# Seven block products in one load of four of the 16-tile products, and running maxima by a matmul

## The chip, the cores and the metric

The kernel runs on one core of a Trainium2 chip. Its metric is the time of one execution in microseconds (us), given as the median of several runs. A core has five engines with instruction queues of their own: PE (TensorE, matmuls), DVE (VectorE), ACT (ScalarE), POOL (GpSimd) and SP (SyncE, which here issues the weight loads). Each engine works its queue in order; semaphores make one wait for another.

## The reference

A decoder trunk of two layers over 256 tokens of width 2048, in float32.

```
xn    = rms_norm(h, g)
q, k, v, o, ig, fg = split(xn @ w_in)               # 8 heads; q, k 128 wide, v, o 256
hh    = mlstm_chunkwise(q, k, v, softcap(ig), log_sigmoid(softcap(fg)))
        # weights exp(dmat - m_t), m_t a running maximum over the tokens;
        # rows divided by max(|sum|, exp(-m_t))
h     = h + (rms_norm(hh, w_hnorm) * sigmoid(o)) @ w_out
h     = h + (silu(conv(up)) * conv(up2)) @ w_down   # gated FFN, width 5632
q     = rope(rms_norm(h, gb) @ w_q);  k, v = split(rms_norm(h, gkv) @ w_kv)
o     = (softmax(q1 k1) - lam * softmax(q2 k2)) @ v # causal, 8 heads, v 256 wide
h     = h + (rms_norm(o, g_subln) * (1 - lambda_init)) @ w_o
h     = h + FFN(h);  out = rms_norm(h, final_norm)
```

The products with "tokens out", which the change is about, are the v and o parts of `xn @ w_in`, `@ w_out`, the v part of `@ w_kv`, and `@ w_o`. Each has 2048 rows of weights, 16 k-tiles of 128, and 2048 columns of output.

## The kernel before

**Arithmetic.** Every float32 operand is split into a high and a low half, `x = xh + xl`, and a product is three matmuls: high by high, low by high, high by low. Weights come from memory as `raw` tiles of one megabyte (four k-tiles of 512 columns; `RAW` = 4 slots). A `granule` takes half of such a tile: ACT copies the high half into a `w2` tile (L375), DVE subtracts it for the low half (L376). There are `HL` = 5 slots for `w2`; a slot comes free when PE has done with the granule in it.

**Products.** `gemm` computes q, k and the FFN's up projections, with columns out. `gemm_tokens` (matmul L436) computes the products with tokens out, in groups of 512 columns: two accumulator banks for a group, one for each 128 tokens, and 16 k-tiles in eight granules of 12 matmuls of 512 columns. `acc_ps` has four accumulator banks, so that two groups can be under way; the other four banks of PSUM (`small_ps`) serve everything small: scores `s_ps`, head outputs `val_ps`, transposes `hn_ps`, `an_ps`, `turn_ps`, and the `mix` banks below. After its last matmul a group is evacuated: `evac_v` scales and splits the values of two heads (`mv`, `av`: ACT L305, DVE L306), `evac_o` multiplies the head rows by the gate, `residual` adds to the residual stream.

**Seven products for eight.** The down projection of the FFN has a second form, `gemm_sevenths` (matmuls L493, ordinary granules L503): for two of the five full loads in each group (a half of the FFN's width is 22 k-tiles) the 2 x 2 block product of (two halves of the tokens, two k-tiles) by (two k-tiles, two column halves) is made with seven block products instead of eight, after Winograd. It needs differences of weight blocks (`sevenths`, DVE L448 to L450, kept in a `diff` tile that takes a slot of `raw`), passes over three and four blocks (L457, L458), four mixed operands for each pair of k-tiles (`mix`, made where the hidden operands are made), and two `mix` banks beside the two accumulators. The sums in the mix banks are added to the stream afterwards by `mixed_in`.

**Heads.** In `mlstm` a head's weights are made in `weights(h)`: scores by L728 and L729, the causal mask minus the running maximum on DVE (L722), three exponentials on ACT (L724 to L726), multiplication by the scores (L730). The running maximum `top[h]` is a row of `mx` that a DMA from POOL's queue broadcasts to 128 partitions (L680), eight of them. `weighted` multiplies with the values (`val_ps`, L334); ACT sums squares (`sq`), DVE and POOL take the inverse root (`rsqrt`: two seeds on DVE, L270 and L271, then three Newton steps of four operations on POOL, L278 to L281), and ACT scales the rows (`hn` in the gated layer, `nrm` in the attention, L347). `turn` transposes them on PE (`hn_ps`, `an_ps`) for the operands of the output projection (`mo`, `ao`).

**Order.** The program is written as Python code in which `later(n, ...)` puts a head's steps behind the n-th next granule (`tick`); from that code a scheduler with a model of the engines' times sets the final order on every engine. The numbers behind names below are buffer numbers.

## Time and profile before

| | |
|---|---|
| median of 3 runs | 2272.68 us (2271.36 to 2272.86) |
| the profiled execution | 2271.45 us, of which the span 2269.6 |
| granted PE clock, mean | 0.997 |
| PE, PEld busy | 2249.4 us, 1948.0 us |
| DVE, ACT, POOL busy | 1699.5 us, 1269.7 us, 120.7 us |
| DMA moved | 420.04 MB, mean 185 GB/s |

PE is busy when a matmul is under way, PEld when PE loads the stationary operand; the two overlap. In a row of a group, "out<-in" are the tiles by the program's names, then counts, busy time and mean, and the engine's idle time ahead with what ended it. The gated layer's products v and o run from about 109 to 304 us of the span, its output projection to about 397, the first FFN to about 1140, the attention's v from 1327 to 1420, its output projection to about 1535, then the second FFN.

### The profile page before, as it was taken

How to read it: one execution, taken by the hardware profiler on the slowest of the kernel's cores; microseconds unless marked ns; L12 is line 12 of the kernel's file. 1: busy time of each engine (PE TensorE's matmuls, PEld its weight loads, DVE VectorE, ACT ScalarE, POOL GpSimd, SP SyncE). 2: the span in 40 equal slices, each digit the busy share in tenths (PEclk: the TensorE clock that was granted, in tenths of full speed). 3: DMA queues.
4: the chain of work that ended last, by engine and by line, in shares of the span. 5: the costliest groups of instructions: out<-in, count | busy, mean ns of one | idle time of the engine just before them, and what ended most of it. 6: DMA issues, size and time to landing. Idle time of an engine off the chain costs nothing.

```text
span 2269.6 us, 32658 instructions
## 1 busy us (share of the span) xinstructions
PE 2249.4 (99%) x12574; PEld 1948.0 (86%) x12574; DVE 1699.5 (75%) x2769; ACT 1269.7 (56%) x1940; POOL 120.7 (5%) x313
## 2 busy tenths in 40 slices
PE   9989999999999999999999999999999999999998
PEld 9868888888888888888888888888888888888888
DVE  6746555778788877788888885567787887787885
ACT  5446544656655555566654556556565555555554
POOL 0013100000000000000012102200000000000000
PEclk9999999999999999999999999999999999999999
DMA  7774555555545755555565555455555466555464
GB/s 264 142 197 161 181 180 182 188 186 186 190 167 185 235 187 186 186 170 183 192 213 188 167 167 167 167 182 181 190 189 186 158 204 214 189 189 191 146 213 149
DMA packets 325728, 420.04 MB, mean 185 GB/s; under 512 B 9198, under 2 KB 238916, under 8 KB 325572
## 3 DMA queue, kind: packets, MB, share of 16 engines
q1 hardware_dynamic: 325156, 416.89, 55.8%
q0 software_dynamic: 384, 1.05, 1.4%
q8 instruction: 99, 1.62, 0.3%
q14 instruction: 57, 0.47, 0.1%
q10 hardware_dynamic: 32, 0.01, 0.0%
HBM read 414.77 MB, written 2.10 MB: 184 GB/s over the span
## 4 chain that ended last, share of the span: by engine, by line
PE 97%; DMA 2%; DVE 0%; ACT 0%; issue 0%; DVEq 0%; ACTq 0%
PE acc L410 53%; PE acc L436 20%; PE acc L503 13%; PE mix L493 4%; PE acc L493 3%; PE acc L594 2%; DMA raw<-in_m_w_in_dram 2%; PE val_ps L334 1%; PE acc L521 1%; PE turn_ps L230 1%; PE as_ps L915 0%; PE gps L641 0%; PE as_ps L916 0%; PE hn_ps L356 0%; PE an_ps L356 0%; PE warm_ps L129 0%
## 5 line engine op out<-in xcount | busy, mean ns | idle before, releaser
L376 DVE TENSOR_TENSOR w<-raw,w 128x1024 fp32r<-128x1024 f32 x708 | 860.1, 1220 | 402.4 <-ACT w L375 398.1
L375 ACT ACTIVATE w<-raw 128x1024 fp32r<-128x1024 f32 x708 | 747.8, 1058 | 596.1 <-PE acc L410 349.3
L410 PE MATMUL acc<-x_f,w 128*128 128x512 f32 (+1 forms) x5632 | 987.9, 337 | 0.0
L410 PEld LDWEIGHTS acc<-x_f,w 128*128 128x128 f32 x5632 | 862.3, 188 | 123.1
L503 PE MATMUL acc<-w,hid 128*128 128x512 f32 x1260 | 299.7, 394 | 0.0
L503 PEld LDWEIGHTS acc<-w,hid 128*128 128x128 f32 x1260 | 233.7, 188 | 52.7
L436 PE MATMUL acc<-w,x_a 128*128 128x512 f32 x768 | 185.8, 399 | 9.1 <-ACT w L375 9.1
L410 PE MATMUL acc<-x_at,w 128*128 128x256 f32 (+1 forms) x1024 | 182.2, 338 | 0.0
L436 PEld LDWEIGHTS acc<-w,x_a 128*128 128x128 f32 x768 | 143.2, 189 | 42.7 <-ACT w L375 9.5
L410 PEld LDWEIGHTS acc<-x_at,w 128*128 128x128 f32 x1024 | 156.8, 188 | 22.4 <-ACT x_at L305 0.3
L416 ACT ACTIVATE low<-acc 128x256 f32<-128x256 f32 x216 | 79.1, 384 | 134.1 <-PE acc L410 134.1
L457 ACT ACTIVATE w<-diff 128x1024 fp32r<-128x1024 f32 x60 | 63.6, 1060 | 92.0 <-PE acc L503 47.4
L417 DVE TENSOR_TENSOR acc<-acc,low 128x256 f32<-128x256 f32 x216 | 84.0, 429 | 40.4 <-ACT low L416 40.3
L796 ACT ACTIVATE c<-u,conv 128x256 f32<-128x256 f32 x176 | 97.9, 593 | 3.5 <-DVE u L794 3.2
L458 DVE TENSOR_TENSOR w<-diff,w 128x1024 fp32r<-128x1024 f32 x60 | 73.2, 1221 | 33.7 <-ACT w L457 33.7
L899 POOL TENSOR_TENSOR sw<-sw,sin_t 32x256 f32<-32x256 f32 x32 | 41.8, 1322 | 1050.3 <-DVE sw L898 1026.6
L436 PE MATMUL acc<-w,ao 128*128 128x512 f32 x384 | 92.0, 396 | 0.0
L436 PE MATMUL acc<-w,x_at 128*128 128x512 f32 x384 | 92.0, 396 | 0.0
L436 PE MATMUL acc<-w,mo 128*128 128x512 f32 x384 | 91.5, 397 | 0.0
L436 PEld LDWEIGHTS acc<-w,mo 128*128 128x128 f32 x384 | 71.4, 188 | 16.7
L436 PEld LDWEIGHTS acc<-w,ao 128*128 128x128 f32 x384 | 71.3, 188 | 16.3
L436 PEld LDWEIGHTS acc<-w,x_at 128*128 128x128 f32 x384 | 71.3, 188 | 16.2
(263 smaller groups left out, 2012.9 us busy)
## 6 DMA issues: line engine op xcount, KB each, us to landing
raw<-in_w_up_dram SPq DMA_DIRECT2D x176, 1024.0 KB
raw<-in_w_down_dram SPq DMA_DIRECT2D x79, 1024.0 KB
raw<-in_m_w_in_dram SPq DMA_DIRECT2D x46, 1024.0 KB
raw<-in_w_kv_dram SPq DMA_DIRECT2D x32, 1024.0 KB
raw<-in_m_w_out_dram SPq DMA_DIRECT2D x16, 1024.0 KB
raw<-in_w_q_dram SPq DMA_DIRECT2D x16, 1024.0 KB
raw<-in_w_o_dram SPq DMA_DIRECT2D x16, 1024.0 KB
raw<-in_w_down_dram SPq DMA_DIRECT2D x15, 512.0 KB
```

Source lines behind the costliest of these rows:

```text
L375: act.activation(w2[:, :hc, 0], part, AF.Copy)
L376: dve.tensor_tensor(w2[:, :hc, 1], part, w2[:, :hc, 0].bitcast(F32), op=ALU.subtract)
L410: pe.matmul(to, a, b, start=(k == 0 and o == 0), stop=(k == kn - 1 and o == len(ops) - 1))
L416: act.activation(low, p[:, T:], AF.Copy)
L417: dve.tensor_tensor(p[:, :T], p[:, :T], low, op=ALU.add)
L436: pe.matmul(ps[t], a[:, s], b, start=(k == 0 and o == 0), stop=(k == kn - 1 and o == 2))
L457: act.activation(w2[:, :n, 0], src, AF.Copy)
L458: dve.tensor_tensor(w2[:, :n, 1], src, w2[:, :n, 0].bitcast(F32), op=ALU.subtract)
L493: pe.matmul(to, u, v, start=start and o == 0, stop=end and o == 2 and to is not a and to is not b, skip_group_check=True)
L503: pe.matmul(ps, u[:, s], v, start=(k0 + i == 0 and o == 0), stop=(k0 + i == kn - 1 and o == 2), skip_group_check=True)
L594: pe.matmul(ps[j], a, b, start=(k == 0 and o == 0 and j % 2 == 0), stop=(k == KD - 1 and o == 2), skip_group_check=True)
L796: act.activation(c, u, AF.Identity, bias=cw[:, 3, f:f + 1], scale=cw[:, 2, f:f + 1])
```

## The change

1. The products v, o, `w_out` and the attention's v go through `gemm_sevenths`, with one load of four k-tiles in seven products: the last load (k-tile 12 on, `MIX_AT[:1]`) for v, o and the attention's v, the third (`OUT_AT[:1]`, k-tile 8 on) for `w_out` and for the last two groups of `w_o`. The first two groups of `w_o` stay in `gemm_tokens`.
2. The operands of that load are mixed: `mix` and a new `mix_scaled` in the normalisation (`Norm.scaled`) and where `mo` and `ao` are made.
3. In v, o and the attention's v the mix banks are added back into the accumulators by a new `mixed_up`, one ACT and six DVE operations, ahead of the evacuation. `residual` uses `mixed_in` as before.
4. The eight broadcasts are gone. The negated maxima of the eight heads stay in rows 0 to 7 (high halves) and 32 to 39 (low halves) of a tile `nm`; `weights(h)` picks a head's row and spreads it with one matmul by `both_r` into a small bank `w_ps`, from which the mask addition and the first exponential read.

Of the 42 matmuls of a load in seven products 18 go into the accumulators and 24 into the two `mix` banks, which are taken from the same four small banks as `w_ps`, `s_ps` and two `val_ps`.

```diff
-            for h in range(HEADS):
-                if h % 2 == 0:
-                    top[h:h + 2] = block(F32, f"top{h // 2}")[:2]
-                nc.gpsimd.dma_start(top[h], mx[h:h + 1].rearrange("p (o t) -> p o t", o=1).broadcast_to([1, P, T]))
+            nm = block(F32R, "nm")[0]
+            pool.memset(nm.bitcast(F32), 0.0)
+            dve.tensor_scalar(nm[:8], mx, -1.0, None, op0=ALU.mult)
+            dve.scalar_tensor_tensor(nm[32:40], mx, -1.0, nm[:8].bitcast(F32), op0=ALU.mult, op1=ALU.subtract)
...
         def weights(h):
             wt = block(F32, "wt")[2][:, :384]
+            w_ps = small_ps("w_ps")[:, :T]
+            pe.matmul(w_ps, both_r[:, h:h + 1].broadcast_to([P, P]), rows["nm"], start=True, stop=True)
...
-            act.activation(wt[:, P:T], top[h][:, P:], AF.Exp, bias=c[:, h:h + 1], scale=-1.0)
+            act.activation(wt[:, P:T], w_ps[:, P:], AF.Exp, bias=c[:, h:h + 1])
...
+    def mixed_up(ps, mix):
+        (a, b), (c, d) = ps, mix
+        u = tmp("mx")
+        x, y = block(F32, "mixed_a"), block(F32, "mixed_b")
+        act.activation(x[1], c[:, :T], AF.Copy)
+        dve.tensor_tensor(u, c[:, T:], x[1], op=ALU.add)
+        dve.tensor_tensor(y[1], d[:, T:], u, op=ALU.add)
+        dve.tensor_tensor(x[0], d[:, :T], u, op=ALU.add)
+        dve.tensor_tensor(y[0], d[:, :T], y[1], op=ALU.add)
+        dve.tensor_tensor(a, a, x[2], op=ALU.add)
+        dve.tensor_tensor(b, b, y[2], op=ALU.add)
...
-        def evac_v(g, ps):
+        def evac_v(g, ps, mix):
+            mixed_up(ps, mix)
...
-        gemm_tokens(xs, w, 2 * HQK, range(4), evac_v)
-        gemm_tokens(xs, w, 2 * HQK + HV, range(4), evac_o)
+        gemm_sevenths(xs, norm.mixed, w, 2 * HQK, range(4), evac_v, MIX_AT[:1])
+        gemm_sevenths(xs, norm.mixed, w, 2 * HQK + HV, range(4), evac_o, MIX_AT[:1])
...
-    gemm_tokens(outs, w_o[0], 0, range(NG), residual(norm_f1), lead=2)
+    gemm_tokens(outs, w_o[0], 0, range(2), residual(norm_f1), lead=2)
+    gemm_sevenths(outs, outs_mixed, w_o[0], 0, range(2, NG), residual(norm_f1), OUT_AT[:1])
```

`mix` itself (four DVE differences, one ACT copy, one DVE low half) is moved, not changed. Lines below L37 move down: L376 becomes L382, L436 in the new form L508, L493 becomes L498, L306 L312, L347 L353.

**What the scheduler makes of it.** The place is the start of the first o group, where the last v group ends. On PE before, the scores of a head stand there, then the granules of the group, each in a `w2` tile of its own slot (2221, 2236 and 2294 lie in three slots):

```order
L728 MATMUL s_ps_2207<-mq3_786,mk3_1248 128x256
L729 MATMUL s_ps_2207<-mq3_786,mk3_1248 128x128
L436 MATMUL acc_2217<-w2_2221,x_a_0_172 128x512 x3
L436 MATMUL acc_2218<-w2_2221,x_a_0_172 128x512 x3
L436 MATMUL acc_2217<-w2_2221,x_a_1_175 128x512 x3
L436 MATMUL acc_2218<-w2_2221,x_a_1_175 128x512 x3
L436 MATMUL acc_2217<-w2_2236,x_a_2_244 128x512 x3
L436 MATMUL acc_2218<-w2_2236,x_a_2_244 128x512 x3
```

Now PE there (`acc_2081` is of the last v group, `acc_2391` and `acc_2392` of the first o group):

```order
L498 MATMUL acc_2081<-w2_2275,x_a_15_650 128x256 x3
L762 MATMUL w_ps_2103<-nm_1003,both_r_116 128x256
L770 MATMUL s_ps_2109<-mq2_811,mk2_1177 128x256
L771 MATMUL s_ps_2109<-mq2_811,mk2_1177 128x128
L508 MATMUL acc_2391<-w2_2395,x_a_0_174 128x512 x3
L508 MATMUL acc_2391<-w2_2395,x_a_1_177 128x512 x3
L508 MATMUL acc_2392<-w2_2395,x_a_0_174 128x512 x3
L508 MATMUL acc_2392<-w2_2395,x_a_1_177 128x512 x3
L508 MATMUL acc_2391<-w2_2430,x_a_2_246 128x512 x2
L508 MATMUL acc_2392<-w2_2430,x_a_2_246 128x512 x2
L340 MATMUL val_ps_2151<-mv4_0_2060,st4_2113 128x258 x2
```

The 18 products of the last v group into its accumulators are ahead of this piece, its 24 products into the mix banks come only after granule 2430; until then the four `w2` tiles 2266, 2269, 2272 and 2275 stay held, and 2395 and 2430 lie in one and the same slot. `acc_2391` and `acc_2392` are the banks that v group 2 had (`acc_1769`, `acc_1770`).

On ACT now, from the evacuation of v group 2 (`mv4`, `mv5`) to the pass for granule 2430:

```order
L311 ACTIVATE mv5_0_2070<-acc_1769,rt_582 128x256
L311 ACTIVATE mv5_1_2073<-acc_1770,rt_582 128x256
L353 ACTIVATE hn3_2099<-val_ps_1988,yh_2014 128x256
L353 ACTIVATE hn3_2099<-val_ps_1992,yh_2014 128x256
L766 ACTIVATE wt_2102<-w_ps_2103,c_col_1031 128x128
L767 ACTIVATE wt_2102<-wt_2102,c_col_1031 128x128
L768 ACTIVATE wt_2102<-wt_2102,c_col_1031 128x128
L381 ACTIVATE w2_2430<-raw_2393 128x2x512
```

The rows of head 3 (`hn3`, which wait for POOL's root) and the exponentials of the next head are ahead of the pass, as they were ahead of another granule's pass before; the granule behind them is now the one that PE needs next.

On DVE before, v group 2 was evacuated in the middle of group 3, between the passes of its second and third loads:

```order
L376 TENSOR_TENSOR w2_2042<-raw_2025,w2_2042 128x2x512
L306 SCALAR_TENSOR_TENSOR mv4_0_1912<-acc_1683,rt_567,mv4_0_1912 128x256
L306 SCALAR_TENSOR_TENSOR mv4_1_1915<-acc_1684,rt_567,mv4_1_1915 128x256
L722 TENSOR_TENSOR wt_1935<-mask_s_126,top2_981 128x2x128
L376 TENSOR_TENSOR w2_2076<-raw_2074,w2_2076 128x2x512
L306 SCALAR_TENSOR_TENSOR mv5_0_1922<-acc_1683,rt_567,mv5_0_1922 128x256
```

Now it stands behind the last seven-product pass of group 3 (w2_2275), and the sums of the mix banks are ahead of it:

```order
L464 TENSOR_TENSOR w2_2275<-diff_2262,w2_2275 128x4x256
L558 TENSOR_TENSOR mx_2050<-mix_1947,mixed_a_2051 128x256
L382 TENSOR_TENSOR w2_2395<-raw_2393,w2_2395 128x2x512
L782 COPY den_2004<-val_ps_1988 128x1
L559 TENSOR_TENSOR mixed_b_2052<-mix_1948,mx_2050 128x256
L560 TENSOR_TENSOR mixed_a_2051<-mix_1948,mx_2050 128x256
L782 COPY den_2004<-val_ps_1992 128x1
L561 TENSOR_TENSOR mixed_b_2052<-mix_1948,mixed_b_2052 128x256
L562 TENSOR_TENSOR acc_1769<-acc_1769,mixed_a_2051 128x512
L783 TENSOR_TENSOR den_2004<-den_2004 128x2
L563 TENSOR_TENSOR acc_1770<-acc_1770,mixed_b_2052 128x512
L784 TENSOR_TENSOR den_2004<-den_2004,e2m_1032 128x2
```

The four splits of `mv4` and `mv5` follow behind this piece, with the two seeds of head 3's root (`yh_2014`) among them.

## The prediction

> **What bounds the kernel now.** I read the page's first and fourth parts, then the waits of PE, then the chain of waits.

> ```profile
> PE 2249.4 (99%) x12574; PEld 1948.0 (86%) x12574; DVE 1699.5 (75%) x2769; ACT 1269.7 (56%) x1940; POOL 120.7 (5%) x313
> PE 97%; DMA 2%; DVE 0%; ACT 0%; issue 0%; DVEq 0%; ACTq 0%
> L376 DVE TENSOR_TENSOR w<-raw,w 128x1024 fp32r<-128x1024 f32 x708 | 860.1, 1220 | 402.4 <-ACT w L375 398.1
> PE acc L436 <- ACT w L375: 9.1, 1, 9.1
> 96.12 37.48 DMA raw<-in_m_w_in_dram
> 133.70 1.06 ACT w L375
> 134.81 1.22 PE acc L436 x2
> ```

> PE is the bound: 97% of the chain and one wait worth the name, 9.1 us. There a weight load of the gated layer takes 37.48 us, the ACT pass follows it, and PE the pass. Whatever takes work off PE is gained in full, unless DVE or ACT then make PE wait. DVE's largest group is a pass of 1.22 us over every weight granule, and DVE sat idle before those passes because ACT, and before ACT the PE, had not released a slot: it has slack, on average 25%.

> **Term 1, the eight broadcasts.** The rows below are the DMA queues from 85 to 135 us, the broadcasts' time to landing, and windows around the stall (span, then busy us of PE, PEld, DVE, ACT, POOL; PEclk; DMA share; GB/s).

> ```profile
> q0 software_dynamic: 384, 1.05, 63.6%
> top<-gate POOLq DMA_DIRECT2D x8, 128.0 KB, 21.8
> 95.00:124.00 29.00, 29.00 (x147) 24.14 (x146) 11.69 (x21) 7.78 (x11) 3.94 (x15) 1.00 0.98 55
> 126.00:128.00 2.00, 0.00 (x0) 0.00 (x0) 0.00 (x0) 0.00 (x0) 0.00 (x0) 0.96 0.92 99
> 128.00:136.00 8.00, 1.19 (x2) 0.50 (x2) 1.21 (x2) 2.00 (x2) 0.00 (x0) 0.50 0.89 268
> 138.00:140.00 2.00, 2.00 (x10) 1.64 (x9) 1.82 (x2) 1.40 (x3) 0.00 (x0) 0.98 1.02 363
> 134.81 5.46 PE L436 MATMUL acc<-w,x_a 128*128 128x512 f32 x15 [9.09 <-ACT w L375]
> ```

> From 95 to 124 us the DMA engines are 98% busy and move 55 GB/s; once the broadcasts are through they move 363. One megabyte in small packets took the engines from the weight loads. Without them nothing is left at this place that PE would wait for, so the 9.1 us go. The granted clock fell to 0.50 in the idle stretch and was still there when PE resumed: 15 matmuls took 5.46 us. At the warm pace below (0.2327 us) they are 3.49, so another 2.0 us go. Term 1: -11.1 (bounds 0, if the load is late for another reason, and -11.1; I take the gain, since the q0 row is the only thing that differs from the windows after). The replacement, a memset, two small DVE operations and eight matmuls of 256 columns, is priced in term 2.

> **Term 2, PE's work.** The down projection already runs such products; its PE timeline:

> ```profile
> 655.59 11.33 PE L503 MATMUL acc<-w,hid 128*128 128x512 f32 x48
> 666.76 0.53 PE L493 MATMUL mix<-w,hid 128*128 128x256 f32 x3
> 671.73 5.72 PE L503 MATMUL acc<-w,hid 128*128 128x512 f32 x24
> 677.29 0.52 PE L493 MATMUL mix<-w,hid 128*128 128x256 f32 x3
> ```

> 48 matmuls of 512 columns take 666.76 - 655.59 = 11.17 us, 0.2327 each. A load of four k-tiles is 24 of them, 5.58 us, or 42 of 256 columns, 671.73 - 666.76 = 4.97. Saved: 0.61 a load, one load in each group: 4 groups of v, 4 of o, 4 of the first output projection, 4 of the attention's v, 2 of its output projection, 18 in all: -11.0. The eight maxima matmuls cost 8 x 0.118 = 0.9. Term 2: **-10.1**. Terms 1 and 2: **-21.2**.

> **Term 3, what DVE and ACT must do more.** Durations from the down projection and from the gated layer (busy us and mean ns behind the bar):

> ```profile
> L448 DVE TENSOR_TENSOR diff<-raw 128x1024 f32<-128x1024 f32 x30 | 36.6, 1219 | 0.4 <-DMA raw<-in_w_down_dram 0.2
> L449 DVE TENSOR_TENSOR diff<-raw,diff 128x512 f32<-128x512 f32 x30 | 20.6, 685 | 0.3
> L458 DVE TENSOR_TENSOR w<-raw,w 128x768 fp32r<-128x768 f32 x60 | 57.1, 951 | 0.8 <-ACT w L457 0.8
> L458 DVE TENSOR_TENSOR w<-diff,w 128x1024 fp32r<-128x1024 f32 x60 | 73.2, 1221 | 33.7 <-ACT w L457 33.7
> L547 DVE TENSOR_TENSOR stream<-acc,stream 128x512 f32<-128x512 f32 x40 | 25.8, 682 | 0.1
> L533 DVE TENSOR_TENSOR mixed<-mix,mixed 128x256 f32<-128x256 f32 x15 | 6.3, 417 | 0.0
> L306 DVE SCALAR_TENSOR_TENSOR mv<-acc,rt,mv 128x256 fp32r<-128x256 f32 x16 | 7.3, 480 | 0.7 <-ACT mv L305 0.4
> 184.00:208.00 24.00, 24.00 (x116) 19.96 (x115) 14.44 (x30) 15.55 (x34) 8.91 (x35) 1.00 0.48 152
> 1019.00:1140.00 121.00, 121.00 (x702) 106.05 (x701) 103.62 (x132) 74.69 (x101) 0.00 (x0) 1.00 0.58 192
> 1327.00:1350.00 23.00, 23.00 (x115) 19.16 (x114) 20.13 (x44) 11.75 (x23) 2.76 (x4) 1.00 0.46 150
> ```

> A group adds on DVE: differences 1.22 + 2 x 0.685 = 2.6; passes 2 x (0.95 + 1.22) instead of 2 x 1.22, 1.9; adding the mixed banks back (L558 to L563) 4 x 0.42 + 2 x 0.68 = 3.0; together 7.5 us in v, o and the attention's v. In a v stage DVE goes from 14.44 to about 22 of 24 us, 91%; in the attention's v, where it has 20.13 of 23, above 100% for one group. The down projection ran at 103.62 of 121, 86%, with no PE wait, but there both loads stand in the middle of a group of 22 k-tiles. The operands' mixes (eight, about 1.9 us of DVE each) are spread over stages with slack, and the loads get more room without q0; both cost nothing as long as DVE has 10% left there.

> Idle DVE is not what decides; the order is. First, in the new order the 24 products into the mix banks are put behind the first one or two granules of the next group. Four of the five w2 slots stay held by then, so granules 0 and 1 of the next group go through one slot (2395 and 2430 both, at the first o group). PE must finish the one before ACT may begin the other: pass 1.06, then DVE behind it, while PE has only the four matmuls that need no low half. Floor: 1.4 us at each of 7 places (v group 3, o groups 0 and 1, attention v groups 1 to 3, its first output group), 9.8 in all. Second, the sums back into the accumulators stand on DVE behind all passes of the next group, and PE's first matmul of the group after that needs them: from the last seven-product pass on, DVE has rows of 1.22 + 4 x 0.42 + 2 x 0.68 + 5 x 0.16 + 3 x 0.48, 6.5 us, against about 0.5 us of PE work. Third, ACT's pass for that one slot is queued behind the head's normalised rows, which wait for POOL:

> ```profile
> 207.67 1.10 POOL L278 TENSOR_TENSOR rs_u<-yh 128x2 f32<-128x2 f32 x1 [0.82 <-DVE yh L271]
> 210.57 0.20 POOL L281 TENSOR_TENSOR yh<-yh,rs_u 128x2 f32<-128x2 f32 x1
> 210.84 1.27 POOL L278 TENSOR_TENSOR rs_u<-yh 128x2 f32<-128x2 f32 x1
> 212.98 0.84 ACT L347 ACTIVATE hn<-val_ps,yh 128x256 f32<-128x256 f32 x2 [2.17 <-POOL mv L715]
> 224.09 0.40 ACT L724 ACTIVATE wt<-top,c_col 128x128 f32<-128x128 f32 x1
> 224.96 1.05 ACT L375 ACTIVATE w<-raw 128x1024 fp32r<-128x1024 f32 x1
> 233.28 0.16 DVE L271 TENSOR_SCALAR yh<-rs_i 128x2 int32<-128x2 int32 x1
> ```

> At o group 0, with zero when DVE ends the last seven-product pass: PE is done at 0.5; accumulators free at 6.5; granule 0 (12 x 0.2327) done at 9.3; the seed of the root, between the sums, at 6.7; POOL 207.67 to 212.98, 5.3, so 12.0; rows 0.84, three exponentials 224.09 to 224.96, 0.87, pass 1.06: 14.8. PE stands 6.0 and then 5.5. DVE runs ahead of PE by 2 to 3 us by my estimate, three slots filled before PE wants them less what is queued there; that leaves about 9 for the place. The same rows stand at o group 1 (8.5). With the same counting: v group 2 0.5, v 3 3.8, o 2 4.5, o 3 2, output projection 1.5; in the attention, where PE's own transposes stand ahead and wait for the root, v groups 1 to 3 4, 4.5 and 6.5, first output group 6.5, later ones 1. Sum about 52. A stall lets DVE and ACT draw level, so the next is shorter; the trace has ACT waiting 2.2 us for POOL before `hn`, not the whole chain. I take three fifths, **+31**. Bounds 0 (cover at every place) and 52.

> **A rule against the change.** POOL's twelve root operations take 0.20 us, but 1.10 and 1.27 where a DVE pass of 1.22 runs. [...] Two of the twelve from 207.67 on were blocked, with DVE 60% busy. Busier by half, it would block about two more, 2.1 us for each chain that PE waits for, and about six are: +13.

> **Sum.** 2271.45 (this execution; 1.2 under the median 2272.68) - 21.2 + 31 = 2281.3; as a median **2282.5**.

> **Rivals.** A measurement of this kernel tells 0.2%, 4.5 us, from no change.
> - Cover holds (faster): DVE and ACT keep the lead that they show in the down projection, and only the one-slot floor is left, up to 17 us with half a pass each: 2272.7 - 21.2 + 9.8 = **2261**. For it: no PE wait there at 86% DVE. Against: slots were never handed from one granule straight to the next. It decides if PE's stalls stay below 17 us.
> - No stall at all, 2251.5: needs every slot free early; the order speaks against it.
> - Halfway, stalls of 17 to 26 us: no change, about **2272**.
> - Stretched chains (slower): POOL's block above, 2282.5 + 13 = **2295.5**. Stalls that last long also cost clock: the 9.09 us above cost 2.0 after it. [...] Four such gaps would be +8 by the row: 2290.5.
> - The change doesn't do what it says: the load at 96 us stays late, +11.1 on any of these. Chance 0.03, within the slower ones.

> **Chances.** Main case, stalls of 26 to 42 us, 0.38 (own range 2277 to 2294); stretched 0.14; halfway 0.13; cover 0.27; no stall 0.08. Slower 0.52, same 0.13, faster 0.35. The range leaves out the no-stall case and the worse half of the stretched one: 2256 to 2301.

> **What would show it.** Term 1: no row of q0, PE's wait at 125 us gone, PEclk 1.00 there. Term 2: 18 more groups of 42 products at 4.97 us, PE's busy time without waits about 10 us lower. Term 3: PE waits on ACT's w pass (new L381) and on DVE's low halves at `mv` and `av` (L312), 3 to 9 us each at the starts of o groups 0 and 1 and in the attention's v, and DVE over 90% from 160 to 300 us. I am wrong if PE's waits sum to under 17 us: then DVE led by more than the 2 to 3 us that I gave it.

## The result and the profile after

The changed kernel takes 2327.67 us (median of 4 runs, 2327.45 to 2327.84) against 2272.05 (2271.36 to 2272.86): slower by a ratio of 1.0244 [1.0228, 1.0260], +55.6 us. The forecast was 2282.5 with a range up to 2301: the sign was right, the size wrong by 45 us. Counted against the -21.2 that terms 1 and 2 promised, 76.8 us of new loss have to be found.

The page after: busy times, the chain that ended last, the one large DMA queue.

```profile
PE 2263.0 (97%) x12906; PEld 1968.2 (85%) x12906; DVE 1825.9 (78%) x3010; ACT 1308.7 (56%) x2017; POOL 127.7 (5%) x306
q1 hardware_dynamic: 325156, 416.89, 54.6%
PE 89%; issue 3%; DVE 3%; POOL 3%; ACT 2%; DMA 1%; SPq 0%; DVEq 0%; POOLq 0%; ACTq 0%
```

PE's share of the chain falls from 97% to 89%, and it is busy for longer although it has less to do. The row of q0 is gone. Next, PE's waits after (tile and line, what ended them; us in total, times, longest):

```profile
PE acc L508 <- ACT w L381: 9.9, 6, 3.0
PE acc L442 <- DVE av L312: 7.2, 2, 5.5
PE spread_ps L299 <- DVE sp_h L294: 6.3, 1, 6.3
PE hn_ps L362 <- DVE o L802: 4.8, 2, 2.5
PE acc L508 <- DVE mv L312: 3.9, 2, 2.0
PE turn_ps L234 <- DVE stream L585: 3.8, 1, 3.8
PE an_ps L362 <- ACT nrm L353: 3.6, 2, 1.9
PE acc L498 <- ACT mix L541: 1.8, 1, 1.8
...
```

All the waits come to 53.9 us, of which 2.3 stood in the profile before as well: 51.6 are new. None comes from a DMA of weights. The rest shows in windows over the stretches in which the granted clock was half (columns as in the prediction's windows; PEclk is the third number from the end). The sum row is over all eight of them; two are shown. The last row is the whole of v and o.

```profile
52.70:59.50 6.80, 3.70 (x9) 2.61 (x10) 3.47 (x7) 1.70 (x4) 0.00 (x0) 0.51 0.55 170
...
346.30:356.50 10.20, 6.42 (x26) 5.57 (x27) 7.48 (x17) 5.32 (x10) 0.00 (x0) 0.51 0.01 2
...
sum 47.60, PE 36.97 PEld 30.31 DVE 24.62 ACT 16.89 POOL 6.07; mean PE 4.62 PEld 3.79 DVE 3.08 ACT 2.11 POOL 0.76
...
116.70:330.90 214.20, 199.81 (x1051) 169.12 (x1049) 154.60 (x264) 117.86 (x215) 45.03 (x144) 0.97 0.46 153
```

PE was busy for 36.97 us at half clock, which is 18.5 us of work at full clock: 18.5 us lost. Before there was one such stretch inside the work, from 127.9 to 138.1 us, in which PE was busy for 3.25. Waits and clock give 70.1 of the 76.8. The other 6.7 lie in PE's busy time: it grew by 13.6 us (2249.4 to 2263.0), where 10.1 less from term 2, 2.0 less from the half clock that went with the old stall, and 18.5 more from the new half clock would make 6.4. They may be the edges of the waits. The row at 214.67 below takes 3.06 us for 12 matmuls that take 2.79 at 0.2327 each, 0.27 more; the 29 new waits at 0.27 would come to 7.8. This is an estimate from one row, and no run isolates it.

The stages can be read from PE's first and last use of the operands of the two output projections, `mo` and `ao` (minimum, median and maximum ns, then first and last start), after:

```profile
L508 PE MATMUL acc<-w,mo x288: 388/394/496, 330.9 to 433.4; 128*128 128x512 f32 x144
L442 PE MATMUL acc<-w,ao x192: 387/394/796, 1474.3 to 1540.1; 128*128 128x512 f32 x192
L508 PE MATMUL acc<-w,ao x144: 388/394/481, 1540.4 to 1586.0; 128*128 128x512 f32 x144
```

The same rows of the other kernels (the experiments are told below) give the stages in us; each column adds up to its kernel's span.

| stage | before | maxima alone | v, o, av | output projections | after |
|---|---|---|---|---|---|
| start, q, k, v, o | 314.5 | 304.3 | 331.1 | 304.3 | 330.9 |
| first output projection | 93.3 | 93.1 | 93.3 | 91.6 | 102.5 |
| FFN, attention's q, k, v | 1025.4 | 1025.8 | 1030.4 | 1031.6 | 1040.9 |
| second output projection | 95.0 | 95.0 | 110.1 | 94.3 | 111.7 |
| the rest | 741.4 | 741.8 | 739.1 | 741.0 | 740.1 |

By these rows v and o end in the kernel before at 314.5 us, and its second output projection begins at 1433.2: some ten us later than the places given ahead of the prediction. Its rows of `x_at` put the attention's v at 1331.3 to 1433.0, so the first 4 us of the prediction's window 1327:1350 belong to the k product.

Three pieces of the timeline after show what a wait is made of. First the start of the first o group (start us, duration, engine and line; the idle time ahead and what ended it in brackets):

```profile
194.66 1.94 PE L498 MATMUL mix<-w,mix 128*128 128x256 f32 x15
199.44 1.10 POOL L284 TENSOR_TENSOR rs_u<-yh 128x2 f32<-128x2 f32 x1 [1.50 <-DVE yh L277]
205.82 0.84 ACT L353 ACTIVATE hn<-val_ps,yh 128x256 f32<-128x256 f32 x2 [2.75 <-POOL mv L755]
206.55 0.39 ACT L557 ACTIVATE mixed_a<-mix 128x256 f32<-128x256 f32 x1
207.91 1.22 DVE L464 TENSOR_TENSOR w<-diff,w 128x1024 fp32r<-128x1024 f32 x1 [3.85 <-ACT w L463]
214.14 0.48 DVE L312 SCALAR_TENSOR_TENSOR mv<-acc,rt,mv 128x256 fp32r<-128x256 f32 x1
214.67 3.06 PE L508 MATMUL acc<-w,x_a 128*128 128x512 f32 x12 [1.97 <-DVE mv L312]
214.77 0.20 POOL L284 TENSOR_TENSOR rs_u<-yh 128x2 f32<-128x2 f32 x1 [0.74 <-DVE yh L277]
218.05 0.84 ACT L353 ACTIVATE hn<-val_ps,yh 128x256 f32<-128x256 f32 x2 [3.51 <-POOL yh L287]
219.61 1.06 ACT L381 ACTIVATE w<-raw 128x1024 fp32r<-128x1024 f32 x1
220.72 2.08 PE L508 MATMUL acc<-w,x_a 128*128 128x512 f32 x4 [3.00 <-ACT w L381]
```

PE waits until the low half `mv` has been taken from the accumulator, then for the pass behind `hn`, which waits for POOL: the chain that the prediction drew. But the mix banks of v group 2 were complete at 196.6 and ACT took them up at 206.55, ten microseconds later, with DVE idle for 3.85 us on the way. On ACT their copy stands right behind the rows `hn` of the head before, and these had waited 2.75 us for POOL, whose chain for that head begins at 199.44.

Second, the start, where the first products wait for the sums of `rms_norm`:

```profile
48.60 0.84 ACT L549 ACTIVATE mx<-turn_ps,gain_a 128x256 f32<-128x256 f32 x2 [0.55 <-DVE x_a L312]
50.53 0.63 ACT L541 ACTIVATE mix<-sum 128x512 fp32r<-128x512 f32 x1 [1.08 <-DVE sum L539]
52.13 2.36 DVE L625 TENSOR_TENSOR w<-raw,w 128x1024 fp32r<-128x1024 f32 x2 [0.25 <-ACT w L624]
54.72 0.45 PE L299 MATMUL spread_ps<-ident_r,sp_h 128*128 128x128 f32 x1 [6.31 <-DVE sp_h L294]
```

The mixes of `x_a` go back and forth between ACT and DVE and stand ahead of weight passes; PE waits 6.31 us, the longest wait of the kernel. Third, the starts of the first FFN and of the last part of the attention:

```profile
445.96 0.66 PE L234 MATMUL turn_ps<-ident,stream 128*128 128x128 f32 x2 [3.82 <-DVE stream L585]
...
1501.94 7.30 PE L442 MATMUL acc<-w,ao 128*128 128x512 f32 x21 [5.51 <-DVE av L312]
```

At both, PE needs what DVE makes last from the final group of a product: the residual stream for the next norm, the low half of the last values.

### The profile page after: what moved, and what is told of

It is laid out like the page before. It is cut to its first block, busy times and chain, and to the rows that moved or that the text cites. A ratio compares the mean times of both kernels' runs of the same rounds, so it can differ in the third digit from the quotient of the medians.

```text
span 2326.1 us, 33628 instructions
## 1 busy us (share of the span) xinstructions
PE 2263.0 (97%) x12906; PEld 1968.2 (85%) x12906; DVE 1825.9 (78%) x3010; ACT 1308.7 (56%) x2017; POOL 127.7 (5%) x306
## 3 DMA queue, kind: packets, MB, share of 16 engines
q1 hardware_dynamic: 325156, 416.89, 54.6%
## 4 chain that ended last, share of the span: by engine, by line
PE 89%; issue 3%; DVE 3%; POOL 3%; ACT 2%; DMA 1%; SPq 0%; DVEq 0%; POOLq 0%; ACTq 0%
PE acc L416 52%; PE acc L508 22%; PE mix L498 5%; PE acc L498 4%; PE acc L442 2%; PE acc L632 1%; DVE w L382 1%; PE acc L526 1%; POOL rs_u L286 1%; POOL rs_u L284 1%; PE turn_ps L234 1%; POOL rs_u L285 1%; POOL yh L287 0%; DVE w L625 0%; ACT w L381 0%
## 5 line engine op out<-in xcount | busy, mean ns | idle before, releaser
L382 DVE TENSOR_TENSOR w<-raw,w 128x1024 fp32r<-128x1024 f32 x672 | 813.7, 1219 | 261.4 <-ACT w L381 258.0
L381 ACT ACTIVATE w<-raw 128x1024 fp32r<-128x1024 f32 x672 | 707.2, 1059 | 500.0 <-PE acc L416 351.1
L508 PE MATMUL acc<-w,hid 128*128 128x512 f32 x1260 | 300.1, 395 | 0.0
L508 PEld LDWEIGHTS acc<-w,hid 128*128 128x128 f32 x1260 | 233.7, 188 | 52.8
L464 DVE TENSOR_TENSOR w<-diff,w 128x1024 fp32r<-128x1024 f32 x96 | 117.2, 1220 | 67.5 <-ACT w L463 67.3
L508 PE MATMUL acc<-w,x_a 128*128 128x512 f32 x576 | 143.8, 406 | 10.4 <-ACT w L381 6.3
L508 PEld LDWEIGHTS acc<-w,x_a 128*128 128x128 f32 x576 | 109.2, 193 | 37.3 <-ACT w L381 7.9
L498 PE MATMUL mix<-w,mix 128*128 128x256 f32 x864 | 121.0, 284 | 0.0
L463 ACT ACTIVATE w<-raw 128x768 fp32r<-128x768 f32 x96 | 81.1, 845 | 69.2 <-PE acc L508 54.2
L498 PEld LDWEIGHTS mix<-w,mix 128*128 128x128 f32 x864 | 111.7, 192 | 0.2
L932 POOL TENSOR_TENSOR sw<-sw,sin_t 32x256 f32<-32x256 f32 x32 | 43.2, 1366 | 1053.6 <-DVE sw L931 1031.6
L464 DVE TENSOR_TENSOR w<-raw,w 128x768 fp32r<-128x768 f32 x96 | 91.3, 951 | 11.3 <-ACT w L463 11.2
L843 DVE SCALAR_TENSOR_TENSOR c<-u,conv,c 128x254 f32<-128x254 f32 x176 | 78.7, 477 | 1.2
L842 DVE SCALAR_TENSOR_TENSOR c<-u,conv,c 128x255 f32<-128x255 f32 x176 | 78.6, 476 | 1.2 <-ACT c L841 1.2
```

What stands on the lines that cost most here:

```text
L381: act.activation(w2[:, :hc, 0], part, AF.Copy)
L382: dve.tensor_tensor(w2[:, :hc, 1], part, w2[:, :hc, 0].bitcast(F32), op=ALU.subtract)
L463: act.activation(w2[:, :n, 0], src, AF.Copy)
L464: dve.tensor_tensor(w2[:, :n, 1], src, w2[:, :n, 0].bitcast(F32), op=ALU.subtract)
L498: pe.matmul(to, u, v, start=start and o == 0, stop=end and o == 2 and to is not a and to is not b, skip_group_check=True)
L508: pe.matmul(ps, u[:, s], v, start=(k0 + i == 0 and o == 0), stop=(k0 + i == kn - 1 and o == 2), skip_group_check=True)
```

## The experiments

Twelve kernels. Diffs are against the changed kernel unless said otherwise; ratios are to the kernel before.

**The maxima alone.** All products go through `gemm_tokens`, no operand is mixed; only item 4 of the change is left.

```diff
-        gemm_sevenths(xs, norm.mixed, w, 2 * HQK, range(4), evac_v, MIX_AT[:1])
+        gemm_tokens(xs, w, 2 * HQK, range(4), evac_v)
...
```

> All products with tokens out as before; only the running maxima by a matmul are kept. Theory 1: the eight broadcasts made the 9.1 us wait and the 2.0 us of half clock behind it, the eight matmuls cost 0.9: 2272 - 10.2 = 2262, no wait of PE at 95 to 135 us and no half clock there. Rival: the weight load at 96 us is late for another reason: 2272 to 2273, with the wait still there.

2261.8 us, 0.9953 [0.9938, 0.9968]. The place of the former stall:

```profile
95.00:124.00 29.00, 29.00 (x145) 23.98 (x144) 16.46 (x26) 11.91 (x15) 0.00 (x0) 1.00 0.57 186
```

The DMA engines move 186 GB/s at 57% where they moved 55 at 98%, and PE's wait is gone. Term 1 holds. The other kernels are read against this one.

**Seven products in v, o and the attention's v alone.** The output projections, `w_o` included, stay in `gemm_tokens`, and their operands are not mixed.

```diff
-    gemm_sevenths(outs, outs_mixed, m_w_out[0], 0, range(NG - 1), residual(norm_f0), OUT_AT[:1])
+    gemm_tokens(outs, m_w_out[0], 0, range(NG - 1), residual(norm_f0))
...
```

> Seven products in v, o and the attention's v only; both output projections as before; maxima by a matmul. Theory 1: every stage pays its own loss. By the starts of the stages in the two traces that is 8 us at the start (operands), 23.6 in v and o less 4.9 saved, 8.7 in the attention's v less 2.4 saved: 2262 + 8 + 18.7 + 6.3 = 2295. Rival: what the output projections and the first FFN lose (11.6, 8.2 and 17.9 us) is a late arrival from v, o and the attention's v: up to 2295 + 34 = 2329.

2306.65 us, 1.0151 [1.0136, 1.0166], +44.9 over the maxima alone: between the two expectations. The table places it: 26.8 from the start to the end of o, where 8 loads should have given back 4.9, nothing in the first output projection, 4.6 up to the second, and 15.1 in the second, whose code was not touched: the late sums and heads of the attention reach into it.

**Seven products in the output projections alone.** The reverse.

> Seven products in the two output projections only (all groups of the first, the last two of the second); v, o and the attention's v as before; maxima by a matmul. Theory 1: each stage pays its own loss: 2262 + 9.2 (first output projection) + 8.2 (start of the first FFN) + 16.7 (second output projection) = 2296. Rival, that these losses are late arrivals from the products ahead: 2262 - 3.7 saved = 2258.

2264.59 us, 0.9966 [0.9953, 0.9979], +2.8 over the maxima alone. Both projections gain (1.5 and 0.7 in the table); 5.8 are lost between them, at the start of the FFN, where PE waits 1.2 us for a pass and this long for the residual stream; the run's mean granted clock was 0.998, where the maxima alone had 0.999:

```profile
PE turn_ps L234 <- DVE stream L585: 3.8, 1, 3.8
```

The theory that the projections' sums hold PE everywhere falls. This and the run before it would add up to 2309.5; the changed kernel takes 18 us more. By the table, 10.7 of these are in the first output projection, 4.7 between the projections, 2.3 in the second. Only with both parts does PE wait there for a mix of `mo` (1.8, the row of `mix` above) and a second time for `o` (2.3 of the 4.8), with the half clock from 346.3 to 356.5 around them.

**The mixes of x_a later, and the mixes alone.** Two runs on the 6.3 us wait at the start: one puts the mixes behind eight granules, one makes them (beside the maxima alone) and uses them nowhere.

```diff
...
+                if self.name == "a":
+                    later(8, lambda: self.mixed.__setitem__(i, mix(pair)))
...
```

> The changed kernel, but the two mixes of the first normalisation's operands are made behind the first product, not inside the part that is kept in the order of the code; their two ACT scalings stay there. Theory: the mixes stand ahead of the weight passes in that order, 2.9 us each on a chain of ACT and DVE, and with the half clock behind the 6.3 us wait they cost 8: of it 6 to 7 come back, 2321. Rival: the start is late for another reason (the operands' ACT scalings, POOL's memset): 2327.

> The maxima-only kernel (2261.8) with the two mixes of the first normalisation's operands made where the changed kernel makes them, and not used. Theory 1: this alone makes the late start of the changed kernel (PE's wait of 6.3 us for the spread of the root and half clock behind it): 2261.8 + 8 = 2270. Rival, after the run with later mixes, which won 2.4 us and lost them again: the start's loss needs the seven-product loads behind it; alone it is 2 to 4, 2265.

The mixes alone cost: 2269.35 us, 0.9988 [0.9979, 0.9997], 7.5 over the maxima alone, with the same wait of 6.3 us and a mean granted clock of 0.997 against 0.999.

```profile
PE spread_ps L299 <- DVE sp_h L294: 6.3, 1, 6.3
```

Putting them later gains nothing: 2329.69 us, 1.0253 [1.0236, 1.0271]. The wait for `sp_h` shrinks to 3.7, but a new one stands in the k product, and v starts at 116.6 us instead of 116.7:

```profile
PE acc L420 <- DVE mk L753: 2.1, 1, 2.1
```

**The sums ahead of the next group's second half.** The passes from k-tile 8 of a group on are ordered behind the sums and the evacuation of the group before, on ACT and on DVE (`SUMS_BY` is 8).

```diff
...
+                    if k0 == SUMS_BY and held:
+                        held["from"] = n
+                        after_sums()
...
```

> The changed kernel with one rule more for the order: in v, o and the attention's v the weight passes from k-tile 8 on stand behind the sums of the group before. Theory 2: the sums stand too late on DVE, since PE had made the mix banks 10 us before ACT began on them; PE's waits for accumulators and gated rows (7.2 + 3.9 + 1.7 for mv and av, 4.8 for o, 1.3 for the scores' bank, 18.9) and some of the half clock go: about 2300. Rival: DVE has no room wherever the sums stand, and the passes put behind them are late instead: PE waits for weight passes grow by as much, 2320 to 2335.

2320.6 us, 1.0214 [1.0200, 1.0228]: 7 less, inside the rival's 2320 to 2335, far from 2300. The waits for `mv` are gone; others have grown:

```profile
PE acc L528 <- ACT w L382: 18.9, 8, 5.1
PE acc L443 <- DVE av L313: 5.5, 1, 5.5
```

What the sums no longer delay, the passes now do: 9.9 us of waiting for a pass became 18.9. So late sums by themselves are not the cause.

**The roots on DVE.** The inverse roots of the heads are computed on DVE instead of POOL.

```diff
-            y = rsqrt(d, "yh", pool)
+            y = rsqrt(d, "yh", dve)
...
```

> The changed kernel with the heads' inverse roots on DVE (nine operations of 0.16 us after the seeds) in place of POOL's twelve. Theory 3: POOL's chain of 3.2 to 5.3 us, which ACT waits for ahead of a weight pass, makes the waits for weight passes and normalised rows (9.9 + 1.3 + 3.6 us): with a chain of about 2 us some 8 us come back with their half clock, 2318. Rival: DVE is the scarce engine; 16 heads at 1.5 us more each cost as much as they give: 2325 to 2335.

2332.27 us, 1.0263 [1.0249, 1.0277]: no gain. The waits for `nrm` (3.6) are gone and those for a pass fall from 9.9 to 7.5, but DVE's own results come later: the waits for `av` grow from 7.2 to 10.5, those for `mv` from 3.9 to 5.8.

```profile
PE acc L442 <- DVE av L312: 10.5, 2, 7.0
```

**The 42 products together.** On PE all products of a seven-product load stand ahead of the next group's first granule, so that four slots are free there instead of one.

```diff
...
+                    if k0 == 0 and products:
+                        behind_products(n)
...
```

> The changed kernel with one rule more for PE's order: in v, o and the attention's v all 42 products of a load stand ahead of the next group's first granule, so that the four weight slots are free before that group begins. Theory 2a: the seven places with one slot cost 11.2 us of waits in the changed kernel (1.69, 3.00, 1.64, 1.21, 1.15, 1.21, 1.27) and what follows them; they go, and the sums can start 5 us earlier: 2305 to 2315. Rival: the mix banks aren't free at that point, since the head's outputs hold them until POOL's root and ACT's rows are done, and PE then waits there, 4 to 5 us a group: 2330 or more.

2340.11 us, 1.0300 [1.0285, 1.0315]. The waits at one slot in v and o are gone, and the whole is 12 us slower. Two rows of PE's waits, then the longest of the three that the profile puts down to "issue":

```profile
PE val_ps L340 <- issue: 15.6, 3, 6.7
PE mix L508 <- ACT hn L353: 4.2, 1, 4.2
...
220.17 0.84 ACT L353 ACTIVATE hn<-val_ps,yh 128x256 f32<-128x256 f32 x2 [3.81 <-POOL yh L287]
222.47 0.61 ACT L326 ACTIVATE st<-wt 128x256 fp32r<-128x256 f32 x2 [0.62 <-DVE wt L788]
222.98 1.20 PE L340 MATMUL val_ps<-mv,st 128*128 128x258 f32 x4 [6.71 <-issue]
```

The wait of 4.2 is the rival's: a mix bank that a head's outputs hold until ACT has made its rows. In the three of 15.6 PE starts 0.1 us after ACT has made the first high half `st` of the next head's weights, and on ACT these stand behind `hn`, which waits for POOL. So the rival had the time right, and most of the waiting is for the weights, not for a bank.

**Short and long waits by themselves.** Into the maxima alone, PE waits were put into the first FFN's products, a chain of small ACT operations that PE must wait for: eight short ones or four long ones, meant to be of about the same idle time together (`GAP_OPS` is 5 and 13).

```diff
...
+        in_turn(pe.transpose(ps[:, :P], ident, ident).ins, last)
+        act.activation(t, ps[:, :32], AF.Copy)
+        for _ in range(GAP_OPS):
+            act.activation(t, t, AF.Copy)
+        return pe.transpose(ps[:32, P:2 * P], t, ident).ins.name
...
```

> The maxima-only kernel (2261.8) with seven waits of PE put into the first FFN's up projection: PE waits for six small ACT operations in a chain, 1.3 to 1.5 us each time. Theory 4, from the clock rows of the changed kernel, where 1.73 us of waiting left the clock alone and 1.88 us halved it: none of these waits changes the clock, and the time is 2261.8 + 7 x 1.5 = 2272. Rival: any wait of PE costs clock behind it: 2280 or more.

> The same with four waits of about 3.1 us (fourteen ACT operations). Theory 4: each is followed by 3.4 or 6.8 us of half clock, which costs 1.7 to 3.4 more: 2261.8 + 4 x 3.1 + 7 to 14 = 2281 to 2288. Rival, that the half clock rows of the changed kernel cost nothing beyond the waits: 2274.

An operation of the chain took longer than expected, so the short waits are 2.5 us instead of 1.4, seven of them (an eighth was filled with other work), the long ones 4.5; their sums, 17.3 and 18.1, are still alike. What a wait of 1.4 us does to the clock these runs do not show. The short kernel took 2283.79 us, 1.0053 [1.0038, 1.0068], the long one 2289.05, 1.0075 [1.0058, 1.0092]: 22.0 and 27.3 over the maxima alone. Waits of the short kernel, then of the long one with a window of it:

```profile
PE gap_ps L404 <- ACT gap_t L403: 17.3, 7, 2.6
```

```profile
PE gap_ps L404 <- ACT gap_t L403: 18.1, 4, 4.5
...
485.90:492.70 6.80, 4.65 (x16) 3.98 (x17) 0.00 (x0) 1.84 (x9) 0.00 (x0) 0.51 0.25 89
```

The clock was half for 6.8 us at the first long wait (the window above), and for 3.4 us behind one short one (817.00 to 820.40, below). The 256 matmuls behind each of the first four short waits took alike, 45.01, 44.99, 44.99 and 45.01 us. Over the run the mean granted clock was 0.994 with the long waits, 0.998 with the short ones and 0.999 with the maxima alone. With 0.55 us of PE for each inserted pair of small matmuls (their durations, 0.27 and 0.28), the short kernel is explained by its waits and its one stretch of half clock, 17.3 + 1.7 + 8 x 0.55 = 23.4 against 22.0. The long one leaves 27.3 - 18.1 - 4 x 0.55 = 7.0 that its waits do not explain, and its granted clock is the lower one. So the clock is a cost of its own. Whether a wait costs something at its edges too these runs cannot tell, since the durations of the pair beside it already hold that; the 6.7 us above stay an estimate.

**What is worth keeping.** The maxima, and seven products only where the covers held: groups 0 to 2 of the first output projection and group 2 of the second. Then the same with two loads a group instead of one.

```diff
-OUT_AT = (8, 10)
+OUT_AT = (4, 6, 8, 10)
...
-    gemm_sevenths(outs, outs_mixed, m_w_out[0], 0, range(NG - 1), residual(norm_f0), OUT_AT[:1])
+    gemm_sevenths(outs, outs_mixed, m_w_out[0], 0, range(NG - 1), residual(norm_f0), OUT_AT[::2])
```

> Maxima by a matmul, and seven products only in groups 0 to 2 of the first output projection and group 2 of the second; the last group of each, whose sums into the stream stand ahead of the next normalisation, in ordinary products. By the stages of the run with output projections only, which won 1.5 and 0.7 us there and lost 6.4 at the start of the first FFN: 2261.8 - 1.1 - 0.4 = 2260.3. Rival: the loss at the start of the FFN doesn't come from the last group: 2264.

> The best kernel so far (2258.85) with a second load of each group in seven products (k-tiles 4 and 8), where DVE has 8 us of idle time in 23. Theory: another 0.61 for each of the four groups: 2256.4. Rival: the two more mixes among the heads' last steps or the longer chain into the stream cost more than they give: 2259 to 2264.

2258.85 us, 0.9942 [0.9928, 0.9955], and 2254.39 us, 0.9922 [0.9908, 0.9937]: the second beats both kernels. Its first output projection:

```profile
L508 PE MATMUL acc<-w,mo x144: 387/393/478, 303.9 to 370.5; 128*128 128x512 f32 x144
L442 PE MATMUL acc<-w,mo x96: 387/394/481, 370.8 to 393.4; 128*128 128x512 f32 x96
```

From 303.9 to 393.4 it takes 89.5 instead of 93.1 with the maxima alone: 3.6 us for six loads, 0.60 each. The two loads of the second projection show no gain (95.2 instead of 95.0). The whole kernel won 7.4, but 2.6 of it is in the rest behind the second projection (739.2 instead of 741.8), which has no new load; the kernel with v, o and av has 739.1 there, so this part is not the loads' doing, and why it varies is not known.

The first of the two also settles the start of the FFN: with the last group of the first projection in ordinary products, the time from that projection to the second is 1026.4 us again, against 1031.6 with that group in seven products.

## Why the prediction was wrong in size

**Term 1 (-11.1, with the matmuls' 0.9) was right.** The maxima alone measured -10.7 (2272.5 to 2261.8), where -10.2 was worked out; q0 and the stall are gone together. The packets of q0 were not small, though: 1.05 MB in 384 are 2.7 KB each, against 1.3 KB in the large queue (416.89 MB in 325156).

**Term 2 (0.61 a load) was right where nothing else waits**, 0.60 in the first projection of the run of two loads a group. In the changed kernel no part of it can be seen, since every stage that should have given it lost more.

**Term 3 had the mechanism, and the size where it was applied.** The floor at seven places with one slot, 9.8, measured 11.2 (1.69, 3.00, 1.64, 1.21, 1.15, 1.21, 1.27). The waits in v, o, the attention's v and `w_o`, for which nearly all of the +31 stood, came to 32.4 (14.3 in v and o, 18.1 behind). That is partly luck: o group 0, worked out as 11.5 and put down as 9, waited 1.97 + 3.00. There POOL's chain took 3.3 us (214.77 to 218.05) and not 5.3, and the pass was through 11.5 us after DVE's last seven-product pass and not 14.8; other places made up for it. The last values of the attention, 5.5 in one wait, were counted less.

**"Cost nothing" for the operands' mixes failed.** They cost 7.5 us at the start, shown by the mixes alone. The step gave busy time, 1.9 us of DVE each, and asked whether DVE has slack. It has; but the two mixes are a chain ACT, DVE, ACT in two queues worked in order, with weight passes behind it, and PE empties its granules meanwhile. Latency in the order was what counted, not the share.

**The output projection at 1.5 and what follows it failed.** There the waits are 6.8 in the first projection (1.1 of it for the load of `conv_b`) and 5.0 at the start of the FFN, with 6.3 of lost clock. The last group's sums stand between the product and the next norm, where no other work is left for PE: the output projections alone show it, at 5.8, and with that group in ordinary products 5.2 of it are gone. The rest appears only when late heads and the mixes of `mo` meet; that it is this meeting is argued from the waits, not shown by a run that separates them.

**The clock was a rival of +8 and belongs in the sum.** It came to 18.5, half of PE's 36.97 busy us in eight stretches. I asked only for waits as long as the one of 9.09 us; waits of 2 to 6 us did it, and one of 1.88 us was enough (below).

**DVE over 90% was wrong, and POOL's slow operations did not add up to the rival's +13.** DVE was busy for 154.60 of 214.20 us, 72%. The stage itself grew, DVE waited in it for ACT (3.85 us in one row), and the work added was less than worked out: from 112.41 us in v and o before, it is 5.3 a group and not 7.5. POOL's chains came out both ways. The one at the start of o group 0 shrank to 3.3 us; the one before it, from 199.44 on, took 6.3, with its first operations at 1.10, 0.79 and 1.05 us beside others of 0.20. Of POOL's 192 root operations 35 took over 0.3 us, 35.3 us together, each beside an operation of DVE; before there were 29, of 30.3 us. The +13 needs about two more in each chain that PE waits for; no run shows them, and the changed kernel has six more in 16 chains. The eight chains of the gated layer come to 42.0 us, before to 41.7, and taking them off POOL gained nothing. Moving the sums, the roots or the products each removed its own wait, and the waits came back elsewhere. That the order of these chains makes the loss, and not the time of one engine, is argued from this and from DVE's 72%, not shown by a run.

Set against the 45 us missed: waits 51.6 instead of 31, +20.6, most of them at the start (7.4), in the first output projection (6.8) and at the start of the FFN (5.0); clock, +18.5; PE's busy time that neither explains, 6.7. Together 45.8.

## What to carry to other kernels

When a rewrite saves a bottleneck engine a little at each place but puts a chain between two other in-order engines there, price the chain's latency where its result is needed next, above all behind the last group of a product, where nothing else is left to run; busy shares say nothing on it. Put such a form only where the result is needed late, and measure it stage by stage: six loads in a quiet stage won 3.6 us, eight in v and o lost 27 with their mixes. And count for each wait of PE of some 2 us or more the half clock that may follow it: here it followed a wait of 1.88 us, and did not follow every one of 2.43.

## What the runs showed of the hardware

```profile
458.64:462.05 3.41, 2.46 (x15) 1.95 (x13) 2.12 (x4) 2.49 (x5) 0.00 (x0) 1.00 0.27 84
462.05:465.46 3.41, 1.94 (x12) 1.70 (x13) 1.22 (x1) 1.26 (x7) 0.00 (x0) 1.00 0.90 299
813.59:817.00 3.41, 0.98 (x8) 0.65 (x7) 1.84 (x2) 2.29 (x7) 0.00 (x0) 1.00 0.43 138
817.00:820.40 3.40, 3.40 (x12) 2.92 (x13) 0.00 (x0) 0.00 (x0) 0.00 (x0) 0.52 0.48 170
```

```profile
1418.10:1421.50 3.40, 1.52 (x9) 1.04 (x8) 2.75 (x3) 0.84 (x2) 2.06 (x2) 0.98 0.00 0
1421.50:1424.90 3.40, 3.40 (x19) 3.40 (x18) 2.17 (x3) 2.48 (x3) 0.00 (x0) 0.52 0.00 0
1472.54:1475.95 3.41, 1.68 (x7) 1.05 (x6) 1.98 (x5) 1.38 (x4) 2.13 (x10) 1.00 0.44 170
342.73:346.14 3.41, 1.75 (x11) 1.14 (x9) 2.17 (x4) 1.79 (x4) 0.00 (x0) 1.00 0.97 315
```

A wait of 2.43 us split over two windows left 2.46 and 1.94 us of work in them and cost no clock; one of the same length inside one window left 0.98, and the next window ran at half. With 1.52 us of work (a wait of 1.88) it was halved too. No sharp limit shows: the window with 1.68 us of work kept the full clock behind it, and the one with 1.75 was followed by the half clock of 346.3 to 356.5. Of all such windows inside the span of the changed kernel that ran at full clock, the eight with 1.54 us of work or less were followed by the half clock; of the six with 1.68 to 1.76, one was.
